# Decay products of an SSD head as two products of 64 targets, all eight heads of a tile in one run

## The chip, the cores and the metric

The kernel runs on one core of a Trainium2 chip. The metric is the device time of one execution in microseconds (us). The core's engines have instruction streams of their own: TensorE (PE in the profile, with its weight loads listed apart as PEld), VectorE (DVE), ScalarE (ACT), GpSimd (POOL) and SyncE (SP), which issues most of the DMAs. An engine takes its instructions in the order in which they stand; between engines, semaphores make one wait for another.

## The reference

A two-layer trunk over 256 positions and 2048 channels: layer 0 mixes with gated DeltaNet heads and band attention, layer 1 with Mamba-2 SSD heads, and each is followed by a squared-ReLU MLP. The change is in the SSD mixer. It has 64 heads of 64 channels in 8 groups; sequences are cut into chunks of 64 positions. The part that matters:

```python
acum = jnp.cumsum(dt * a, axis=2)
xdt = x * dt[..., None]
a_t = jnp.moveaxis(acum, 2, -1)
decay = jnp.exp(jnp.where(causal, a_t[..., :, None] - a_t[..., None, :], -jnp.inf))
cb = jnp.einsum('bnlgs,bnmgs->bnglm', cm, bm)
y_diag = jnp.einsum('bngelm,bnmgep->bnlgep', cb[:, :, :, None] * decay, xdt)
# a scan over the chunks adds y_off, then
y = y_diag + jnp.moveaxis(y_off, 0, 1) + x * d_skip.reshape(SSD_GROUPS, SSD_HPG, 1)
```

For each head, y_diag is a product of a matrix of weights (source position by target position: decay times cb) with the head's inputs (source position by 64 channels). All values are float32.

## The kernel before, in words

The 256 positions are handled as two tiles of 128, so the kernel's chunk is 128 positions where the reference's is 64; the formula allows either. Large projections run on TensorE all the time: their weights come in 1 MB pieces by DMA (`raw`, L499), ScalarE rounds each half to float32r (`wh`, L332), VectorE takes the remainder (`wl`, L336), and TensorE multiplies with both (L322). Between these products the code of a mixer is woven in.

`ssd_group` (L1378) is the code of one group of eight heads. It is a generator: each `yield` hands control back to the loop that emits the projections, so that a step of it is written every few products. It fetches the decay rows (`sE`, L1392, four heads in a [128, 4, 128] tile, four such tiles a group), computes cb (`scb`), transposes x (`sx`) and multiplies it by dt (L1437), and then works through four steps: tile 0 heads 4 to 7, tile 0 heads 0 to 3, and the same for tile 1. `weights` (L1415) makes the products' weights of one step out of a decay tile: a minimum on VectorE (L1418), four exponentials on ScalarE (L1420), the product with cb on VectorE (L1421). One step behind, the decay products of four heads run on TensorE: for each head, 128 source positions by 128 targets as weights, and as moving columns this head's 64 and, except for head 0, the 64 of the head before it, whose own product is written over that part next. All eight heads of a tile go into one PSUM tile `py`; behind head 0 VectorE adds the other terms and writes `y` (L1461, L1462). `ssd_gate` (L1466) reads `y` later.

`self.mm` (L325) is the call for all float32 products; a float32 product is two records of weight load and two of product in the profile. Other narrow products in the kernel: the cumulative sums of dt (L1357, float32, 64 weight columns, tile `sd_A`), the transposes of the 64 rows that come of it (`sd_rows`, L1365), and the dt projection (L667 and L668, float32r, by turns 128 and 64 weight columns, tile `wn`).

The order in which instructions stand on each engine is set when the program is built, by a scheduler that starts from the order of emission, the dependencies and the number of buffers of each pool. The pool of PSUM tiles `pm` has four, the pool of SBUF tiles that holds `sE`, `sx`, `scb` and others 18, `wl` five.

Of the kernel before, what the change touches and what calls it, by code (L numbers as in the profile page):

```python
# [14 lines left out]
ALU = mybir.AluOpType  # L15
# [3 lines left out]
P = 128  # L19
# [47 lines left out]
def wait(*tasks):  # L67
    for t in tasks:
        while not t.done:
            yield False  # L70
# [42 lines left out]
class Trunk:  # L113
# [933 lines left out]
    def gdn_tile(self, hg, t, kf, qf, vf, G):  # L1047
# [35 lines left out]
        self.mm(ps.rearrange("p h i -> p (h i)"), self.SU, gu.rearrange("p h i -> p (h i)"))  # L1083
        E = self.s2(tag="gE")
        nc.scalar.activation(E, ps, AF.Exp)
        nc.vector.tensor_tensor(E, E, self.row(self.U), op=ALU.mult)
        yield
# [12 lines left out]
        for h in range(4):  # L1100
            nc.vector.scalar_tensor_tensor(lt[:, h], ps[:, h], be[:, h : h + 1], E[:, h], op0=ALU.mult, op1=ALU.mult)

# [7 lines left out]
        p1 = self.s2(tag="gPt")  # L1110
        nc.vector.tensor_tensor(p1, ps, E, op=ALU.mult)
        G["Pt", t] = p1
# [265 lines left out]
    def ssd_group(self, g, xc, Bc, Cc, dtc):  # L1378

        nc = self.nc  # L1380
        yield from wait(xc, Bc, Cc, dtc())
        yield
        xf = xc.result
        H = slice(g * 8, g * 8 + 8)
        B, C = Bc.result[:, g % 4], Cc.result[:, g % 4]
        steps = [(t, hh) for t in range(2) for hh in (1, 0)]

        def decay(t, hh):

            E = self.s2(tag="sE")  # L1390
            h0 = g * 8 + hh * 4
            nc.scalar.dma_start(E, self.s_rows[t, h0 : h0 + 4].unsqueeze(0).to_broadcast([P, 4, P]))  # L1392
            return E

        Es = [decay(*n) for n in steps]
        ps = self.pm()
        for t in range(2):
            T = slice(t * P, t * P + P)
            self.mm(ps[:, t], B[:, T], C[:, T])
        self.mm(ps[:, 2], B[:, :P], C[:, P:])  # L1400
        cb = self.s2([P, 3, P], tag="scb")
        nc.vector.tensor_tensor(cb[:, :2], ps[:, :2], self.row(self.U, 2), op=ALU.mult)
        nc.scalar.copy(cb[:, 2], ps[:, 2])
        yield
        xt = []
        for t in range(2):
            ps = self.pm()
            for f in range(4):
                self.tr(ps[:, f], xf[:, f, t * P : t * P + P])
            x = self.s2([P, 8, 64], tag="sx")  # L1410
            nc.scalar.copy(x.rearrange("p h d -> p (h d)"), ps.rearrange("p f d -> p (f d)"))
            xt.append(x)
            yield

        def weights(t, hh, E):  # L1415

            h0 = g * 8 + hh * 4
            nc.vector.tensor_tensor(E, E, self.bc(self.s_col[:, t, h0 : h0 + 4]), op=ALU.min)  # L1418
            for h in range(4):
                nc.scalar.activation(E[:, h], E[:, h], AF.Exp, bias=self.s_ncol[:, t, h0 + h : h0 + h + 1])  # L1420
            nc.vector.tensor_tensor(E, E, self.row(cb[:, t]), op=ALU.mult)  # L1421
            return E


        xw = self.s2([P, 8, 64], tag="sxw")
        nc.vector.tensor_tensor(xw, xt[0], self.bc(self.s_dr[:, H], 64), op=ALU.mult)
        yield
        ps = self.pm([P, 8, 64])
        self.mm(ps.rearrange("p h d -> p (h d)"), cb[:, 2], xw.rearrange("p h d -> p (h d)"))
        yo = self.s2([P, 8, 64], tag="syo")  # L1430
        nc.vector.tensor_tensor(yo, ps, self.bc(self.s_ec[:, H], 64), op=ALU.mult)

        xds = []
        for t in range(2):
            xds.append(self.s2([P, 8, 64], tag="sxd"))
            nc.vector.tensor_tensor(xds[t], xt[t], self.bc(self.s_d[:, H], 64), op=ALU.mult)
            nc.vector.tensor_tensor(xt[t], xt[t], self.bc(self.dt[:, t, H], 64), op=ALU.mult)  # L1437
        y = self.unit(shape=[P, 2, 8, 64])
        yield
        py, E = None, None  # L1440
        for n in range(5):
            Ep = E
            if n < 4:
                E = weights(*steps[n], Es[n])
            if n == 0:
                yield
                continue
            t, hh = steps[n - 1]


            xf2 = xt[t].rearrange("p h d -> p (h d)")
            if hh == 1:
                py = self.pm([P, 512])
            for h in (3, 2, 1, 0):
                hl = hh * 4 + h
                s = slice(max(hl - 1, 0) * 64, hl * 64 + 64)
                self.mm(py[:, s], Ep[:, h], xf2[:, s])
            if hh == 0:
                xd = xds[t]
                if t == 1:  # L1460
                    nc.vector.tensor_tensor(xd, xd, yo, op=ALU.add)  # L1461
                nc.vector.tensor_tensor(y[:, t].rearrange("p h d -> p (h d)"), py, xd.rearrange("p h d -> p (h d)"), op=ALU.add)  # L1462
            yield
        return y

    def ssd_gate(self, g, ps, task):  # L1466
# [367 lines left out]
```

## Time and profile before

| | |
|---|---|
| time, median of 3 runs | 2707.59 us (2705.99 to 2708.86) |
| profiled execution | 2705.89 us |
| its span | 2704.0 us |
| mean granted TensorE clock | 0.993 |
| busy: PE, PEld, DVE | 2646.9, 2337.1, 2155.6 us |
| busy: ACT, POOL | 1348.6, 24.2 us |
| HBM read | 675.33 MB |
| decay products (`pm<-sx,sE`) on TensorE | from 1397.0 to 1828.9 us |

The profile is of one execution; its own time is 2705.89 us, of which 2704.0 are between the first and the last instruction. Products on TensorE are pipelined and their ends are modelled, so that records of products that follow each other overlap; how fast they go is read from their starts. In a row such as `L325 PE MATMUL pm<-sx,sE 128*128 128x64 f32`, `pm` is what is written, `sx` and `sE` what is read, 128*128 are rows and columns of the array that hold weights, and 128x64 are partitions and moving columns. The SSD groups lie in two places, four groups each, because the groups are worked through in two halves with an output projection behind each.

### The profile page before, as it was taken

How to read it: one execution, taken by the hardware profiler on the slowest of the kernel's cores; microseconds unless marked ns; L12 is line 12 of the kernel's file. 1: busy time of each engine (PE TensorE's matmuls, PEld its weight loads, DVE VectorE, ACT ScalarE, POOL GpSimd, SP SyncE). 2: the span in 40 equal slices, each digit the busy share in tenths (PEclk: the TensorE clock that was granted, in tenths of full speed). 3: DMA queues.
4: the chain of work that ended last, by engine and by line, in shares of the span. 5: the costliest groups of instructions: out<-in, count | busy, mean ns of one | idle time of the engine just before them, and what ended most of it. 6: DMA issues, size and time to landing. Idle time of an engine off the chain costs nothing.

```text
span 2704.0 us, 39515 instructions
## 1 busy us (share of the span) xinstructions
PE 2646.9 (98%) x15578; PEld 2337.1 (86%) x15578; DVE 2155.6 (80%) x3106; ACT 1348.6 (50%) x1990; POOL 24.2 (1%) x98
## 2 busy tenths in 40 slices
PE   5999999999999999999999999999999999999999
PEld 4887989888888888888888888888888888888888
DVE  7998998998888888889889876996787855555554
ACT  3444555455355354454556544655555354454452
POOL 1000000000000000000000000000000000000000
PEclk7999999999999999999999999999999999999999
DMA  9986487867899889988556665555557855555553
GB/s 350 354 326 235 169 313 266 317 248 284 315 348 329 334 326 334 331 326 300 181 182 212 224 234 203 203 179 180 196 187 290 323 201 190 187 187 187 188 193 133
DMA packets 100457, 680.05 MB, mean 251 GB/s; under 512 B 11184, under 2 KB 14512, under 8 KB 19376
## 3 DMA queue, kind: packets, MB, share of 16 engines
q1 hardware_dynamic: 95376, 669.07, 68.2%
q10 hardware_dynamic: 4896, 8.46, 1.1%
q8 instruction: 122, 2.00, 0.3%
q14 instruction: 63, 0.52, 0.1%
HBM read 675.33 MB, written 2.16 MB: 251 GB/s over the span
## 4 chain that ended last, share of the span: by engine, by line
PE 87%; DVE 7%; DMA 3%; ACT 2%; issue 1%; SPq 0%; ACTq 0%; DVEq 0%
PE pw L322 66%; PE pg L322 13%; PE pm L325 4%; PE pm L322 2%; DVE mraw L456 2%; DVE wl L336 2%; DMA mraw<-in_mod_dram 2%; PE pm L329 1%; DMA raw<-in_wo_ab_dram 1%; ACT wh L332 0%; DVE u L1614 0%; DVE hf L883 0%; DMA raw<-in_w_ab_dram 0%; DVE x L948 0%; ACT pm L1065 0%
## 5 line engine op out<-in xcount | busy, mean ns | idle before, releaser
L336 DVE TENSOR_TENSOR wl<-raw,wh 128x1024 fp32r<-128x1024 f32 x870 | 1051.0, 1220 | 440.0 <-ACT wh L332 437.3
L332 ACT CAST wh<-raw 128x1024 fp32r<-128x1024 f32 x870 | 905.6, 1051 | 991.4 <-PE pw L322 690.1
L322 PE MATMUL pw<-u,wh 128*128 128x512 f32 x5584 | 1321.2, 391 | 2.9 <-DVE x L948 1.5
L322 PEld LDWEIGHTS pw<-u,wh 128*128 128x128 f32 x5584 | 1031.7, 188 | 208.7 <-DVE x L948 1.5
L322 PEld LDWEIGHTS pw<-u,wl 128*128 128x128 f32 x5584 | 702.4, 191 | 22.7 <-issue 1.6
L322 PE MATMUL pw<-u,wl 128*128 128x256 f32 x5584 | 713.8, 283 | 1.5 <-DVE wl L336 0.7
L456 DVE SCALAR_TENSOR_TENSOR mraw<-mraw,crow 128x2048 f32<-128x2048 f32 x192 | 438.1, 2283 | 12.8 <-DMA mraw<-in_mod_dram 12.8
L322 PE MATMUL pg<-wh,u 128*128 128x512 f32 x864 | 281.8, 397 | 0.0
L322 PEld LDWEIGHTS pg<-wh,u 128*128 128x128 f32 x864 | 162.1, 188 | 32.3 <-issue 0.5
L948 DVE SCALAR_TENSOR_TENSOR x<-pw,mod,x 128x256 f32<-128x256 f32 x352 | 161.3, 478 | 32.7 <-PE pw L322 30.2
L322 PE MATMUL pg<-wl,u 128*128 128x512 f32 x432 | 169.6, 393 | 0.3
L322 PE MATMUL pg<-u,wh 128*128 128x256 f32 x672 | 124.5, 285 | 0.0
L322 PEld LDWEIGHTS pg<-u,wh 128*128 128x128 f32 x672 | 105.5, 192 | 0.3
L322 PEld LDWEIGHTS pg<-wl,u 128*128 128x128 f32 x432 | 81.3, 188 | 17.2 <-DVE wl L336 1.7
L322 PE MATMUL pg<-u,wl 128*128 128x256 f32 x336 | 95.5, 284 | 0.0
L322 PE MATMUL pm<-u,wh 128*128 128x256 f32 (+1 forms) x340 | 63.5, 291 | 19.2 <-ACT wh L332 19.2
L322 PEld LDWEIGHTS pm<-u,wh 128*128 128x128 f32 x340 | 53.9, 198 | 20.3 <-ACT wh L332 20.0
L322 PEld LDWEIGHTS pg<-u,wl 128*128 128x128 f32 x336 | 64.4, 192 | 0.0
L1007 DVE SCALAR_TENSOR_TENSOR u<-pad,cst,u 128x256 f32<-128x256 f32 x144 | 60.2, 477 | 4.4 <-ACT u L1001 4.3
L885 ACT ACTIVATE u<-hf,mod 128x256 fp32r<-128x256 f32 x64 | 29.3, 502 | 50.6 <-DVE hf L883 50.6
L1520 ACT COPY rs<-pw 128x512 f32<-128x512 f32 x64 | 36.9, 577 | 34.5 <-PE pw L322 34.5
L1526 ACT ACTIVATE rl<-rs 128x512 f32<-128x512 f32 x64 | 40.5, 633 | 23.7 <-DVE rs L1521 21.0
(298 smaller groups left out, 1556.0 us busy)
## 6 DMA issues: line engine op xcount, KB each, us to landing
raw<-in_w_dram SPq DMA_DIRECT2D x256, 1024.0 KB, 5.1
mraw<-in_mod_dram SPq DMA_DIRECT2D x192, 1024.0 KB, 6.2
raw<-in_w_ab_dram SPq DMA_DIRECT2D x56, 1024.0 KB, 5.4
raw<-in_w_ssd_dram SPq DMA_DIRECT2D x48, 1024.0 KB, 4.9
raw<-in_w_sz_dram SPq DMA_DIRECT2D x32, 1024.0 KB, 4.9
raw<-in_wo_ssd_dram SPq DMA_DIRECT2D x32, 1024.0 KB, 4.9
raw<-in_wo_ab_dram SPq DMA_DIRECT2D x16, 1024.0 KB, 7.0
sE<-sd_rowd ACTq DMA_DIRECT2D x32, 256.0 KB, 4.5
```

Of the source, the lines that this page charges most:

```text
L322: return self.nc.tensor.matmul(o, a, b, start=start, stop=stop, skip_group_check=True)
L325: self.nc.tensor.matmul(o, lhsT, rhs, start=True, stop=True, skip_group_check=True)
L329: return self.nc.tensor.transpose(o, a, self.anti if flip else self.ident[:k, :k])
L332: a = self.nc.scalar.copy(hi, src)
L336: b = self.nc.vector.tensor_tensor(lo, src, hi.bitcast(F32), op=ALU.subtract)
L456: x = nc.vector.scalar_tensor_tensor(raw, raw, 1.0, self.crow, op0=ALU.mult, op1=ALU.mult, accum_out=t[:, f : f + 1])
L885: nc.scalar.activation(hi, h[:, f], AF.Identity, bias=shift[:, col])
L948: self.last = nc.vector.scalar_tensor_tensor(x[:, 2 * b + f], ps[:, f, n], g[:, 2 * cb + f : 2 * cb + f + 1], x[:, 2 * b + f], op0=ALU.mul ...
L1007: nc.vector.scalar_tensor_tensor(h, pad[:, f, 1 + q : 257 + q], w[:, q, j : j + 1], h, op0=ALU.mult, op1=ALU.add)
L1520: nc.scalar.copy(lo, ps[:, :, 1])
L1526: nc.scalar.activation(rl, lo, AF.Relu)
```

## The change

The loop over five half-tile steps becomes a loop over the two tiles. For a tile it first makes the weights of heads 4 to 7 and then of heads 0 to 3, with a `yield` behind each as before. Then it takes a PSUM tile and writes the products of all eight heads in one run. Each head is two products: targets 0 to 63 and targets 64 to 127, each with all 128 sources, 64 weight columns and the head's 64 channels as moving columns. The first writes partitions 0 to 63 of `py`, the second partitions 64 to 127, which stand for the two column halves of the array. No head writes over another's columns any more. The y addition follows at once, in the same step, ahead of the weights of the next tile. The number of yields stays five.

```diff
         yield
-        py, E = None, None
-        for n in range(5):
-            Ep = E
-            if n < 4:
-                E = weights(*steps[n], Es[n])
-            if n == 0:
+        for t in range(2):
+            E = []
+            for hh in (1, 0):
+                E.insert(0, weights(t, hh, Es[2 * t + 1 - hh]))
                 yield
-                continue
-            t, hh = steps[n - 1]
-
-
-            xf2 = xt[t].rearrange("p h d -> p (h d)")
-            if hh == 1:
-                py = self.pm([P, 512])
-            for h in (3, 2, 1, 0):
-                hl = hh * 4 + h
-                s = slice(max(hl - 1, 0) * 64, hl * 64 + 64)
-                self.mm(py[:, s], Ep[:, h], xf2[:, s])
-            if hh == 0:
-                xd = xds[t]
-                if t == 1:
-                    nc.vector.tensor_tensor(xd, xd, yo, op=ALU.add)
-                nc.vector.tensor_tensor(y[:, t].rearrange("p h d -> p (h d)"), py, xd.rearrange("p h d -> p (h d)"), op=ALU.add)
-            yield
+            py = self.pm([P, 512])
+            for h in range(8):
+                c = slice(h * 64, h * 64 + 64)
+                for i in (slice(0, 64), slice(64, P)):
+                    self.mm(py[i, c], E[h // 4][:, h % 4, i], xt[t][:, h])
+            xd = xds[t]
+            if t == 1:
+                nc.vector.tensor_tensor(xd, xd, yo, op=ALU.add)
+            nc.vector.tensor_tensor(y[:, t].rearrange("p h d -> p (h d)"), py, xd.rearrange("p h d -> p (h d)"), op=ALU.add)
+        yield
         return y
```

TensorE in the first group of heads, tile 0, before. `pm` is the PSUM tile of the decay products, `sE` the weights (12880 heads 4 to 7, 12882 heads 0 to 3), `pw` the projection that runs meanwhile; the size is that of what is written, and x4 is four products.

```order
L322 MATMUL pw_13050<-u_12055,wh_12972 128x512 x3
L325 MATMUL pm_13035<-sx_12920,sE_12880 128x128 x4
L322 MATMUL pw_13050<-u_12055,wh_12972 128x512
L322 MATMUL pw_13050<-u_12056,wh_12972 128x512 x4
L325 MATMUL pm_13035<-sx_12920,sE_12882 128x128 x3
L325 MATMUL pm_13035<-sx_12920,sE_12882 128x64
L322 MATMUL pw_13050<-u_12088,wh_12976 128x512 x4
```

The same place now:

```order
L322 MATMUL pw_13045<-u_12055,wh_12972 128x512 x4
L322 MATMUL pw_13045<-u_12056,wh_12972 128x512 x4
L325 MATMUL pm_13054<-sx_12920,sE_12882 64x64 x8
L325 MATMUL pm_13054<-sx_12920,sE_12880 64x64 x8
L322 MATMUL pw_13045<-u_12088,wh_12976 128x512 x4
```

Two runs of four products became one run of sixteen, which stands where the second run stood; the first four heads moved behind five products of the projection, and heads 0 to 3 now come first.

TensorE in the same group, tile 1, before:

```order
L322 MATMUL pw_13050<-u_12089,wl_12977 128x256 x4
L325 MATMUL pm_13091<-sx_12942,sE_12884 128x128 x4
L322 MATMUL pw_13050<-u_12136,wl_13043 128x256 x4
L322 MATMUL pw_13050<-u_12137,wl_13043 128x256 x4
L322 MATMUL pw_13050<-u_12184,wl_13047 128x256 x3
L325 MATMUL pm_13091<-sx_12942,sE_12886 128x128 x3
L325 MATMUL pm_13091<-sx_12942,sE_12886 128x64
L322 MATMUL pw_13050<-u_12184,wl_13047 128x256
L322 MATMUL pw_13050<-u_12185,wl_13047 128x256 x4
```

and now:

```order
L322 MATMUL pw_13045<-u_12184,wl_13042 128x256 x4
L322 MATMUL pw_13045<-u_12185,wl_13042 128x256 x4
L322 MATMUL pw_13045<-u_12136,wh_13037 128x512 x4
L322 MATMUL pw_13045<-u_12137,wh_13037 128x512 x4
L325 MATMUL pm_13123<-sx_12942,sE_12886 64x64 x8
L325 MATMUL pm_13123<-sx_12942,sE_12884 64x64 x8
L322 MATMUL pw_13045<-u_12184,wh_13041 128x512 x4
```

The run of tile 1 moved behind the rest of the projection's 256-wide products and eight of its 512-wide ones.

VectorE between the weights of tile 0 and the y addition of tile 1, before (L1462 adds y, L1418 and L1421 are the two steps of the weights, L336 makes wl):

```order
L336 TENSOR_TENSOR wl_13043<-raw_13040,wh_13042 128x1024
L336 TENSOR_TENSOR wl_13047<-raw_13040,wh_13046 128x1024
L1418 TENSOR_TENSOR sE_12884<-sE_12884,sd_col 128x512
L1462 TENSOR_TENSOR u_12998<-pm_13035,sxd_12992 128x512
L996 TENSOR_TENSOR pad_13078<-pw_12906,cvt_13079 128x2x256
L1418 TENSOR_TENSOR sE_12886<-sE_12886,sd_col 128x512
L1421 TENSOR_TENSOR sE_12884<-sE_12884,scb_12892 128x512
L1007 SCALAR_TENSOR_TENSOR u_12895<-pad_13078,cst,u_12895 128x256 x4
L1421 TENSOR_TENSOR sE_12886<-sE_12886,scb_12892 128x512
```

and now (L1453 is the y addition):

```order
L336 TENSOR_TENSOR wl_13038<-raw_13035,wh_13037 128x1024
L336 TENSOR_TENSOR wl_13042<-raw_13035,wh_13041 128x1024
L1453 TENSOR_TENSOR u_12998<-pm_13054,sxd_12992 128x512
L1418 TENSOR_TENSOR sE_12884<-sE_12884,sd_col 128x512
L996 TENSOR_TENSOR pad_13086<-pw_12906,cvt_13087 128x2x256
L1418 TENSOR_TENSOR sE_12886<-sE_12886,sd_col 128x512
L1452 TENSOR_TENSOR sxd_12995<-sxd_12995,syo_12990 128x512
L336 TENSOR_TENSOR wl_13145<-raw_13142,wh_13144 128x1024
L1421 TENSOR_TENSOR sE_12884<-sE_12884,scb_12892 128x512
L1007 SCALAR_TENSOR_TENSOR u_12895<-pad_13086,cst,u_12895 128x256 x2
L1421 TENSOR_TENSOR sE_12886<-sE_12886,scb_12892 128x512
L1007 SCALAR_TENSOR_TENSOR u_12895<-pad_13086,cst,u_12895 128x256 x4
```

The y addition of tile 0 moved ahead of the first weights of tile 1, and one split (wl) moved ahead of their second step.

## The prediction

> **What bounds the kernel now.** I read the page first: busy time by engine, then the chain of work that ended last.
>
> ```profile
> PE 2646.9 (98%) x15578; PEld 2337.1 (86%) x15578; DVE 2155.6 (80%) x3106; ACT 1348.6 (50%) x1990; POOL 24.2 (1%) x98
> PE 87%; DVE 7%; DMA 3%; ACT 2%; issue 1%; SPq 0%; ACTq 0%; DVEq 0%
> ```
>
> TensorE is busy 98% of the span and carries 87% of the chain. That is an average, so next come the windows around the changed place: the decay products run from 1397 to 1829 us, four head groups in the first two windows and four in the last two. Two windows of the MLP behind them are added. The columns are window, its length, then busy time and instructions of PE, PEld, DVE, ACT and POOL, the granted clock, the DMA share and GB/s.
>
> ```profile
> 1390.00:1480.00 90.00, 90.00 (x526) 77.67 (x525) 88.67 (x137) 56.55 (x110) 0.62 (x6) 1.00 0.59 204
> 1480.00:1560.00 80.00, 79.70 (x390) 66.70 (x390) 67.06 (x114) 43.77 (x67) 0.00 (x0) 1.00 0.60 218
> 1560.00:1740.00 180.00, 180.00 (x1045) 158.93 (x1044) 135.48 (x197) 90.42 (x120) 0.72 (x7) 1.00 0.61 215
> 1740.00:1840.00 100.00, 100.00 (x568) 85.78 (x567) 90.07 (x143) 59.51 (x111) 0.31 (x3) 1.00 0.54 178
> ...
> 2150.00:2350.00 200.00, 200.00 (x1154) 177.11 (x1153) 117.00 (x133) 92.94 (x104) 0.00 (x0) 1.00 0.57 204
> 2350.00:2550.00 200.00, 200.00 (x1154) 177.14 (x1153) 111.89 (x124) 97.46 (x112) 0.00 (x0) 1.00 0.54 190
> ```
>
> Between 1390 and 1840 us TensorE idles for 0.3 us. So time on TensorE's stream there is time of the kernel, one to one. The rest of the program is filled by TensorE in the same way, with DMA at about half, so a gain here is not given back behind. One thing to watch is VectorE (DVE): 88.67 of 90 us in the first window. Busy time of pipelined products overlaps, so the price of a product has to come from starts, not from durations.
>
> **What a decay product costs now.** TensorE's rows in order of time in the first group, one row of its weight loads, and a piece of the chain:
>
> ```profile
> 1397.02 1.05 PE L325 MATMUL pm<-sx,sE 128*128 128x128 f32 x8
> 1397.83 1.39 PE L322 MATMUL pw<-u,wh 128*128 128x512 f32 x5
> 1399.06 1.00 PE L325 MATMUL pm<-sx,sE 128*128 128x128 f32 x8
> 1399.87 2.10 PE L322 MATMUL pw<-u,wh 128*128 128x512 f32 x8
> ...
> 1398.83 1.08 PEld L325 LDWEIGHTS pm<-sx,sE 128*128 128x128 f32 x8
> ...
> 1397.18 0.89 PE pm L325 x8
> ```
>
> One run is four products and x8 records: an fp32 product is two passes, each with its own weight load. The chain gives 0.89 us for eight passes, 0.111 each. All records of this product, by shape, and the narrow weight loads that the kernel has elsewhere:
>
> ```profile
> L325 PEld LDWEIGHTS pm<-sx,sE x256: 186/192/192, 1396.8 to 1828.9; 128*128 128x128 f32 x128
> L325 PE MATMUL pm<-sx,sE x256: 222/275/348, 1397.0 to 1828.9; 128*128 128x128 f32 x112, 128*128 128x64 f32 x16
> ...
> L322 PEld LDWEIGHTS pg<-u,wn 128*64 128x64 f32 x16 | 2.1, 134 | 0.0
> L325 PEld LDWEIGHTS pm<-Ucmask,sd_A 128*64 128x64 f32 x4 | 0.4, 136 | 0.5 <-DVE sd_A L1350 0.5
> ```
>
> 256 passes at 0.111 are **28.5 us**, which is all that the change can touch directly. The durations are min/median/max in ns. A product with 64 moving columns shows 222 where one with 128 shows 275: 64 columns are 53 ns of streaming. A load of 64 weight columns shows 134 to 136, one of 128 shows 192: 64 columns are about 56 ns of loading. Loading and streaming both take about 106 to 112 ns per pass now and lie over each other; that is the 0.111.
>
> **The change, part by part.** *Added passes.* Each head becomes two products of 64 weight columns and 64 moving columns, so 512 passes take the place of 256. One such pass alone needs 53 ns plus the 5 ns by which 0.111 exceeds 2 x 53: 58 ns. If the two halves of the array work at the same time, two passes fit in 58, so 29 ns each, 512 x 0.029 = 14.8 us. If passes still follow each other, 512 x 0.058 = 29.7 us. If load and product no longer overlap, 55 + 53 = 108 ns, 55.3 us. No row of this kernel shows two halves in use together: these are the bounds. I take 29 ns, with little confidence: the products of consecutive instructions share neither weights nor output partitions, and the only thing known to be common is the path of the loads.
>
> *Entering and leaving the narrow form.* The kernel has one fp32 product with 64 weight columns already, the cumulative sums of dt. TensorE's rows there, and then those of its weight loads:
>
> ```profile
> 1369.88 0.65 PE L325 MATMUL pm<-Ucmask,sd_A 128*64 128x128 f32 x4 [0.32 <-DVE sd_A L1350]
> 1370.46 1.22 PE L322 MATMUL pw<-u,wl 128*128 128x256 f32 x8
> 1371.61 0.33 PE L329 MATMUL pm<-ident,sd_rows 64*128 64x64 f32 x2
> ...
> 1370.46 1.01 PEld L322 LDWEIGHTS pw<-u,wl 128*128 128x128 f32 x8 [0.17 <-issue]
> ...
> 1401.80 2.07 PE L322 MATMUL pw<-u,wl 128*128 128x256 f32 x16
> 1403.71 1.06 PE L325 MATMUL pm<-sx,sE 128*128 128x128 f32 x8
> ```
>
> Of the row at 1369.88 the first load takes 0.056 (above) and four passes stream 128 columns each, 2 x 53 ns apiece: streaming ends near 1370.36. The next weight load, which waits for nothing that the profile shows, starts at 1370.46, nearly 0.1 later. Its eight products then take 1.22 us, where the steady rate of the row at 1401.80, 0.119 a pass, gives 1.12. So leaving costs 0.1 of nothing and 0.1 of a load that no product covers: about 0.20. Entering is seen at 1371.61 (a 64-row transpose): the row ahead ends at 1371.68 by its record, and a next product starts 0.07 ahead of that end, where in the steady row it starts 0.16 ahead (2.07 + 1401.80 - 1403.71); again 0.09, and then an uncovered load, 0.055 for 64 columns. Together **0.35 us for a run**. The old 128-wide runs pay none of it: 0.81 from 1397.02 to the next product at 1397.83. There are 16 new runs (8 groups, 2 tiles), so 5.6 us. The other bound is zero, from the dt projection, whose one-pass products alternate between 128 and 64 weight columns:
>
> ```profile
> 1338.96 3.90 PE L322 MATMUL pg<-u,wn 128*128 128x256 f32 x32
> 1342.69 0.63 PE L322 MATMUL pw<-u,wh 128*128 128x512 f32 x2
> ```
>
> 32 passes in 3.73 us are 0.117 each, the steady rate. I take 5.6, because the sums of dt are the same kind of product (fp32, two passes) and the projection is not. The Trainium skill ("TensorEngine Tiling (Array Packing)", Key Properties) says that changing the tiling mode drains TensorE: the sums of dt agree with it, the projection's row does not, and by the rule every change of width would pay, which leaves the sum at 5.6.
>
> *Moved work.* Heads of one tile now run together, so the first four wait for the last four. In the first group the run of tile 0 stands behind eight 512-wide products instead of three, that of tile 1 behind all 32 of the 256-wide ones and eight 512-wide. VectorE, same place:
>
> ```profile
> 1396.95 0.68 DVE L1421 TENSOR_TENSOR sE<-sE,scb 128x512 f32<-128x512 f32 x1
> ...
> 1404.41 0.68 DVE L1421 TENSOR_TENSOR sE<-sE,scb 128x512 f32<-128x512 f32 x1
> ...
> 1405.92 1.00 PE L325 MATMUL pm<-sx,sE 128*128 128x128 f32 x8
> ```
>
> Weights of tile 0 are done at 1397.63; its run starts five 512-wide products behind 1397.02, which is 1.23 (1397.83 to 1399.06), so near 1398.2. Weights of tile 1 were done at 1405.1; the y addition and one split now stand ahead of them on VectorE (0.6 and 1.2 us), so 1406.9. Its run starts behind five more 256-wide products than the second old run (0.6) and eight 512-wide ones (1.9, from 1399.87 to 1401.80), so about 2.4 us after 1405.92, near 1408.3. No wait on TensorE: 0. The y addition of tile 1 is the reverse: VectorE reaches it about when that run ends, and what stands behind it are the splits of the next weights (wl) and the next group's masks. That can cost VectorE about 1 us a group. It would first have to use up the lead that wl has over its first use. The least that I find between 1390 and 1480 us is this split, done at 1465.01 and used at 1468.66:
>
> ```profile
> 1463.79 1.22 DVE L336 TENSOR_TENSOR wl<-raw,wh 128x1024 fp32r<-128x1024 f32 x1
> ...
> 1468.66 0.40 PE L322 MATMUL pg<-wl,u 128*128 128x512 f32 x1
> ```
>
> That is 3.6 us, against about 1 us in each of the three groups up to there. I put it at 0, at most 1 us.
>
> *Sum:* 14.8 + 5.6 - 28.5 = **-8.1 us**. The profiled execution took 2705.9 us (span 2704.0), so 2697.8; the median of the three runs is 1.7 above the profiled one: **2699.5**.
>
> **The rivals.**
>
> *Passes in turn (slower).* The loads of the two halves go one after the other on one path, as they do now. Place: the weight loads inside the 16 runs; price 58 ns a pass, 29.7 + 5.6 - 28.5 = +6.8 us, 2714.4. It decides as soon as a pass costs more than (28.5 - 5.6) / 512 = 45 ns. For it: in every row today a load starts only when the product ahead has started. Against: with one set of spare weights that is seen either way.
>
> *Half of it.* Loads partly side by side, 43.5 ns a pass: 22.3 + 5.6 - 28.5 = -0.6, 2707.0. The work is halved and the runs' edges eat it.
>
> *No overlap of load and product.* 108 ns a pass: 55.3 + 5.6 - 28.5 = +32.4, 2740.0. Against: the eight loads from 1398.83 lie under products that use all rows. The Trainium skill ("TensorE: Matmul & The Clock Gate", Part 3) says a load overlaps products in flight only where the row groups differ, and both halves use all rows; the trace disagrees for full-width products, and no run here shows the halves. The same part reports 2.38 times for three column tiles, which is for the forecast.
>
> *Edges cost nothing*, as in the dt projection: 14.8 - 28.5 = -13.7, 2693.9.
>
> **How the numbers follow.** Forecast 0.36 (2699.5, its own range 2697 to 2703 for 28 to 36 ns a pass), edges free 0.06, half 0.17, in turn 0.33, no overlap 0.08. What this kernel can tell from no change is about 0.2%, 5.4 us. Faster is the forecast and the free edges, 0.42. Within 0.2% is the half and a little of the passes in turn, 0.19; slower the rest, 0.39. The range takes in all but the last rival and the tails: 2692 to 2718.
>
> **What would show it.** In the changed kernel's trace TensorE's run of a tile should hold 32 records of 64-wide form. From its first start to the next wide product, about 1.0 us means halves at once, about 1.9 means in turn, 3.5 no overlap. The first wide load behind each run should start with a gap of 0.09. TensorE's waits for sE should stay at none, and VectorE's for the y addition should be the only new ones. The forecast is wrong if a pass costs over 45 ns, or if wl comes late on TensorE between 1390 and 1480 us.

## The result and the profile after

The changed kernel takes 2697.5 us (median of 5 runs, 2696.3 to 2699.49) against 2706.27 for the kernel before on the same chip (5 runs, 2704.61 to 2708.86): a ratio of 0.9964 with a 95% interval of 0.9953 to 0.9975, or 8.8 us less, 6.8 to 12.7 by the interval. The profiled execution has a span of 2695.8 us where the one before had 2704.0, which is 8.2 less. The forecast was 8.1 less, 2699.5 us; of the 2.0 us by which it is off, 1.3 lie in the time of the kernel before, of which it knew a median of 2707.59.

The page's busy times by engine and its chain of work, of the changed kernel:

```profile
PE 2638.6 (98%) x15834; PEld 2325.0 (86%) x15834; DVE 2154.2 (80%) x3106; ACT 1348.0 (50%) x1990; POOL 24.4 (1%) x98
PE 91%; DVE 5%; DMA 1%; ACT 1%; issue 1%; SPq 0%; ACTq 0%; DVEq 0%
```

TensorE has 256 more records of product and 256 more of weight load, as expected of 512 passes in place of 256, and is busy 8.3 us less. Still 98% busy, it bounds the kernel as before. The windows around the changed place, in the columns of the prediction:

```profile
1390.00:1480.00 90.00, 89.87 (x637) 75.19 (x637) 87.89 (x136) 56.07 (x107) 0.62 (x6) 1.00 0.58 203
1480.00:1560.00 80.00, 79.56 (x430) 65.75 (x429) 70.28 (x118) 45.47 (x75) 0.00 (x0) 1.00 0.64 235
1560.00:1740.00 180.00, 180.00 (x1089) 158.66 (x1088) 135.27 (x198) 90.95 (x118) 0.73 (x7) 1.00 0.60 213
1740.00:1840.00 100.00, 100.00 (x671) 83.19 (x670) 90.95 (x144) 60.89 (x114) 0.31 (x3) 1.00 0.53 187
```

TensorE idles for 0.57 us in them, where it was 0.30. So the time went out of its stream and not out of waits. TensorE's products in order of time in the first group, then its weight loads at the first run:

```profile
1393.69 5.40 PE L322 MATMUL pw<-u,wh 128*128 128x512 f32 x23
1399.01 1.15 PE L325 MATMUL pm<-sx,sE 128*64 128x64 f32 x32
1400.10 2.11 PE L322 MATMUL pw<-u,wh 128*128 128x512 f32 x8
1402.04 4.00 PE L322 MATMUL pw<-u,wl 128*128 128x256 f32 x32
1405.88 2.00 PE L322 MATMUL pw<-u,wh 128*128 128x512 f32 x8
1407.81 1.15 PE L325 MATMUL pm<-sx,sE 128*64 128x64 f32 x32
1408.89 2.11 PE L322 MATMUL pw<-u,wh 128*128 128x512 f32 x8
...
1399.01 1.01 PEld L325 LDWEIGHTS pm<-sx,sE 128*64 128x64 f32 x32 [0.35 <-ACT cvt L995]
1400.09 1.69 PEld L322 LDWEIGHTS pw<-u,wh 128*128 128x128 f32 x8
```

A run holds 32 passes and takes 1.09 us from its first start to the next product of the projection (1399.01 to 1400.10); before, eight passes took 0.81, and a tile had two such runs. All records of the decay products, their count, min/median/max of the durations in ns, and the shape, whose count is of a sample of every third record:

```profile
L325 PEld LDWEIGHTS pm<-sx,sE x512: 132/138/138, 1399.0 to 1821.5; 128*64 128x64 f32 x171
L325 PE MATMUL pm<-sx,sE x512: 222/222/271, 1399.0 to 1821.5; 128*64 128x64 f32 x171
```

The durations are those of narrow forms in the profile before (134 to 136 for a load of 64 columns, 222 for a product with 64 moving columns): a pass has not become shorter, two of them stand side by side. In the starts of the single records of the first run the weight loads come in pairs, at 1399.012 and 1399.019, 1399.067 and 1399.074, 1399.124 and 1399.130 and so on: the second of a pair 6 to 7 ns behind the first, and one pair every 58 ns. That is 29 ns a pass.

To follow the gain along the program, the start of the same product of the projection was compared in the two traces. From 1392 us, ahead of the first run, to 1842, behind the last, the changed kernel gains 8.1 us; from there to the end 0.9 more. That is one wait that went: near 2083 us TensorE of the kernel before waits for ScalarE to round `u` (0.68 of idle time), and in neither profile of the changed kernel does it. Why it went was not taken apart. Ahead of 1392, where nothing changed, two profiled executions of this same kernel lie 0.8 and 3.3 us behind the one before, so single spans are good to some 3 us and the stretch is the better measure.

### The profile page after: what moved, and what is told of

The parts are those of the page before. It is cut to its first block, busy times and chain, and to the rows that moved or that the text cites. A ratio compares the mean times of both kernels' runs of the same rounds, so it can differ in the third digit from the quotient of the medians.

```text
span 2695.8 us, 40020 instructions
## 1 busy us (share of the span) xinstructions
PE 2638.6 (98%) x15834; PEld 2325.0 (86%) x15834; DVE 2154.2 (80%) x3106; ACT 1348.0 (50%) x1990; POOL 24.4 (1%) x98
## 4 chain that ended last, share of the span: by engine, by line
PE 91%; DVE 5%; DMA 1%; ACT 1%; issue 1%; SPq 0%; ACTq 0%; DVEq 0%
PE pw L322 71%; PE pg L322 13%; PE pm L325 3%; PE pm L322 2%; DVE mraw L456 2%; PE pm L329 1%; DVE wl L336 1%; DMA mraw<-in_mod_dram 1%; DVE u L1605 0%; ACT wh L332 0%; DVE hf L883 0%; DMA raw<-in_w_ab_dram 0%; DVE u L886 0%; DMA x<-in_x_dram 0%; DMA sd_rowd<-sd_rows 0%
## 5 line engine op out<-in xcount | busy, mean ns | idle before, releaser
L336 DVE TENSOR_TENSOR wl<-raw,wh 128x1024 fp32r<-128x1024 f32 x870 | 1050.8, 1220 | 435.9 <-ACT wh L332 433.1
L1512 DVE TENSOR_TENSOR rs<-pw,rs 128x512 f32<-128x512 f32 x64 | 43.8, 684 | 10.0 <-ACT rs L1511 10.0
```

The lines of the kernel that those rows point to most:

```text
L336: b = self.nc.vector.tensor_tensor(lo, src, hi.bitcast(F32), op=ALU.subtract)
L1512: nc.vector.tensor_tensor(lo, ps[:, :, 0], lo, op=ALU.add)
```

## The experiments

They change `ssd_group` of the changed kernel, except two: the halves in runs of four heads start from the kernel before, and the last one changes the dt projection. To compare runs of different length, each run is priced in the same way, from the starts of single records: from the last 512-wide product of the projection ahead of it to the second one behind it, less the 0.46 us that two such products take at their steady rate (eight in 1.93 from 1405.88, with the 0.10 gap ahead of the run in it, is 0.229 each). Before, a run of eight passes costs 0.892 by this (1.352 less 0.46), 28.5 us for 32; in the changed kernel a run of 32 costs 1.275, 20.4 us for 16. Runs between 256-wide products, priced with 0.119 for each of those, cost the same (0.897 and 1.275).

### The same regrouping with products of full width

All eight heads of a tile in one run, each head one product of 128 targets and its own 64 channels; no column halves.

```diff
-                for i in (slice(0, 64), slice(64, P)):
-                    self.mm(py[i, c], E[h // 4][:, h % 4, i], xt[t][:, h])
+                self.mm(py[:, c], E[h // 4][:, h % 4], xt[t][:, h])
```

> The changed kernel, but each head is one product of all 128 targets and 64 moving columns; the run of eight heads and the order of the work stay. If two halves of the array working at once make the gain: back to the time before, 2706 (256 passes at 0.111 = 28.5 us, bound by the load of 128 weight columns, and no edges), within 2 us. If it comes from the regrouping into one run or from the moved additions: 2698, as the changed kernel. If it comes from moving 64 columns in place of 128: under 2700 as well, and starts of passes 58 ns apart in the trace in place of 111.

Measured: 2706.06 us against 2706.39, ratio 1.000 (0.9991 to 1.001). TensorE's first run:

```profile
1397.70 1.89 PE L325 MATMUL pm<-sx,sE 128*128 128x64 f32 x16
1399.40 2.10 PE L322 MATMUL pw<-u,wh 128*128 128x512 f32 x8
```

16 passes take 1.70 us to the next product. In the starts of single records one follows the other every 0.112 us, as before: the load of 128 columns sets that pace and not the stream, which is half as long now. The run costs 1.786, twice the 0.892 of eight passes. So the regrouping and the halved moving columns, without the halves, are worth nothing by the runs' prices, and at most 2.4 us by the times; what gains is the halves.

### The halves one after the other

The same products, all eight lower halves of a tile first and then the eight upper ones.

```diff
-            for h in range(8):
-                c = slice(h * 64, h * 64 + 64)
-                for i in (slice(0, 64), slice(64, P)):
+            for i in (slice(0, 64), slice(64, P)):
+                for h in range(8):
+                    c = slice(h * 64, h * 64 + 64)
```

> The changed kernel with the same 16 products a run in another order: the lower half of all eight heads, then the upper half of all eight. If the gain is two halves at once and the queue doesn't look eight products ahead: passes 58 ns apart, 1.9 us a run in place of 1.0, about 0.85 x 16 = 13.5 us over the changed kernel, 2711. If narrower products are what gains, in whichever order: 2697.5, starts 29 ns apart on average.

Measured: 2708.7 us against 2706.39, ratio 1.001 (1.0001 to 1.0019).

```profile
1399.94 1.90 PE L325 MATMUL pm<-sx,sE 128*64 128x64 f32 x32
1401.77 2.11 PE L322 MATMUL pw<-u,wh 128*128 128x512 f32 x8
```

The same 32 records, in 1.83 us and not 1.09. Passes of one half start 58 ns apart. This is the rival "passes in turn" as a kernel: a pass costs the 58 ns that it was priced at, the kernel is slower than before, and the change escapes it only because the two halves alternate. The run is a little below 32 in turn (32 x 0.058 and the 0.15 of leaving are 2.01): in the starts of single loads a second series sets in at 1400.690, when two of the first sixteen are still to come, and three passes overlap. That is 0.18 a run, and it takes the rival's 6.8 us down to 3.9.

### Each product twice

Every product is written a second time, which changes nothing in the output.

```diff
-                for i in (slice(0, 64), slice(64, P)):
+                for i in (slice(0, 64), slice(64, P)) * 2:
```

> The changed kernel with each product written twice (lower, upper, lower, upper of each head; the second pair repeats the first). Measures the price of a pass in time: 512 passes more. At 29 ns: +14.8 us over the changed kernel, 2712. At 58: +29.7, 2727. If the runs are hidden behind something else: under +5, 2702.

Measured: 2709.8 us against 2706.39, ratio 1.001 (1.0001 to 1.002); 12.2 us more than the changed kernel's difference.

```profile
1394.98 2.09 PE L325 MATMUL pm<-sx,sE 128*64 128x64 f32 x64
1397.00 2.11 PE L322 MATMUL pw<-u,wh 128*128 128x512 f32 x8
```

64 passes take 2.02 and 32 take 1.09: 32 more passes in 0.93, which is 29 ns each. This is the marginal price of a pass, free of the run's edges. By the runs' cost (2.208 each) the kernel should be 6.8 us slower than before; the time says 3.4, at most 5.4 by the interval. The traces show what lies between them. In the stretch from 1392 to 1842 the kernel loses 5.6: 6.8 for the runs, less 0.5 for waits that the kernel before has in four of its runs and this one does not have, less 0.46 for the kernel before's wait at 1499, which it does not have either (both are shown further below), is 5.8. Behind 1842 it loses 0.9 less, by the same wait at 2083 that went in the changed kernel. That leaves 4.7, inside the interval. Ahead of 1392, where nothing changed, this execution is 3.3 us early.

### Halves in runs of four heads

The loop of the kernel before, with its 32 runs of four heads, but two half products for a head.

```diff
-                s = slice(max(hl - 1, 0) * 64, hl * 64 + 64)
-                self.mm(py[:, s], Ep[:, h], xf2[:, s])
+                s = slice(hl * 64, hl * 64 + 64)
+                for i in (slice(0, 64), slice(64, P)):
+                    self.mm(py[i, s], Ep[:, h, i], xf2[:, s])
```

(The removed lines are those of the kernel before.)

> The loop of before, two runs of four heads a tile, with the products of the change in it. 16 runs more, so 16 edges more. If entering and leaving cost 0.35 us a run: +5.6 us over the changed kernel, 2703. If edges cost nothing: 2697.5. If the places of the runs matter more than their edges (weights come late, as in the kernel before): over 2705.

Measured: 2703.9 us against 2706.39, ratio 0.9992 (0.9983 to 1.0002).

```profile
1397.53 0.69 PE L325 MATMUL pm<-sx,sE 128*64 128x64 f32 x16
1398.15 1.42 PE L322 MATMUL pw<-u,wh 128*128 128x512 f32 x5
```

A run of 16 passes takes 0.62 to the next product and costs 0.810. With the changed kernel's 1.275 for 32, a pass is 29.1 ns once more, and what is left of a run without its passes, 1.275 less 32 x 0.0291, is **0.344 us** for entering and leaving. The prediction had 0.35. Sixteen more runs at that price take 5.5 of the 8.1 us: in the old grouping the halves alone would hardly have been seen, and the regrouping, worth nothing by itself, is what pays for the halves' edges.

### The changed kernel again, and both tiles in one run

If edges cost 0.34 a run, half as many runs should gain 2.75 us. In the last kernel of this group all four steps of weights come first, then one run of 32 products, tile 1 ahead of tile 0, and then both y additions (left out of the cut below). Its companion is the changed kernel, once more.

```diff
+        Ew = {}
         for t in range(2):
-            E = []
             for hh in (1, 0):
-                E.insert(0, weights(t, hh, Es[2 * t + 1 - hh]))
+                Ew[t, hh] = weights(t, hh, Es[2 * t + 1 - hh])
                 yield
-            py = self.pm([P, 512])
+        pys = [self.pm([P, 512]) for _ in range(2)]
+        for t in (1, 0):
             for h in range(8):
...
-                    self.mm(py[i, c], E[h // 4][:, h % 4, i], xt[t][:, h])
+                    self.mm(pys[t][i, c], Ew[t, h // 4][:, h % 4, i], xt[t][:, h])
```

> The changed kernel itself, as the partner of the next kernel on the same chip: 2697.5, 0.9964 of before.

> The changed kernel with both tiles of a group in one run of 32 products (tile 1 first); weights of all four steps are made before it. 8 runs in place of 16, so 8 edges fewer. If an edge costs 0.35 us: 2.8 us under the changed kernel, 2694.7. If the later run delays VectorE's additions and with them wl or the gates: no gain, or over 2697.5, with waits of TensorE for wl or u in the trace. If edges are free: 2697.5.

Measured, against 2706.14: the changed kernel 2697.79 us, ratio 0.9967 (0.9955 to 0.9979); both tiles in one run 2695.48 us (2693.03 to 2696.65), ratio 0.9958 (0.9946 to 0.9971). TensorE's run of the first group:

```profile
1406.50 2.09 PE L325 MATMUL pm<-sx,sE 128*64 128x64 f32 x64
1408.52 1.88 PE L322 MATMUL pw<-u,wh 128*128 128x512 f32 x7
```

Eight runs of 2.208 are 17.7 us, 10.8 less than before, and 10.7 were measured. By the medians it is 2.3 us ahead of the changed kernel, near the 2.75 of the edges; the two intervals overlap, so that this step rests on the runs' lengths more than on the times. It has the lowest median of this study.

The runs' costs and the times side by side, in us against the kernel before:

| kernel | runs | cost of one | sum less 28.5 | measured (95%) |
|---|---|---|---|---|
| changed | 16 | 1.275 | -8.1 | -8.8 (-12.7 to -6.8) |
| changed, again | 16 | 1.275 | -8.1 | -8.4 (-12.2 to -5.7) |
| full width, one run | 16 | 1.786 | +0.1 | -0.3 (-2.4 to +2.7) |
| halves in turn | 16 | 2.025 | +3.9 | +2.3 (+0.3 to +5.1) |
| each product twice | 16 | 2.208 | +6.8 | +3.4 (+0.3 to +5.4) |
| halves, four heads | 32 | 0.810 | -2.6 | -2.5 (-4.6 to +0.5) |
| both tiles in one run | 8 | 2.208 | -10.8 | -10.7 (-14.6 to -7.8) |

### What the edges hang on

The prediction saw two cases that disagree: the sums of dt pay for the narrow form, the dt projection does not. They differ in more than one thing. Here the dt projection's narrow product is made in float32, two passes, as the sums of dt are; its neighbours stay float32r and 128 wide. The same line makes a projection of layer 0, which is changed with it; nothing else is.

```diff
-                self.mmx(o[:width, :SEQ], w[:, :width], u[:, k % 2, 1], False, k == 15)
+                self.mmx(o[:width, :SEQ], w[:, :width].bitcast(F32), u[:, k % 2, 1].bitcast(F32), False, k == 15)
```

> The changed kernel; in the dt projection (and the gates' projection) the narrow product of each step is float32 in place of float32r, with the same 64 (16) weight columns, so that it alternates with float32r products of 128 (32) columns. If it is the float32 form that makes the switch cost, the 32 switches in the dt projection show the gap of 0.09 us and an uncovered load each, and the 32 products take about 16 x (0.117 + 0.44 + 0.35) = 14.5 us in place of 3.7. If only what follows decides (a change of width as such), 16 x (0.117 + 0.44) = 8.9 us and no gaps.

Measured, one run: 2715.68 us. The projection in TensorE's products, in this kernel, and some of its weight loads there:

```profile
1347.91 14.24 PE L322 MATMUL pg<-u,wn 128*128 128x256 f32 x48
1362.09 3.93 PE L322 MATMUL pw<-u,wh 128*128 128x512 f32 x16
...
1347.69 0.19 PEld L322 LDWEIGHTS pg<-u,wn 128*128 128x128 f32 x1
1348.12 0.19 PEld L322 LDWEIGHTS pg<-u,wn 128*64 128x64 f32 x2 [0.24 <-issue]
1348.70 0.51 PEld L322 LDWEIGHTS pg<-u,wn 128*128 128x128 f32 x3 [0.39 <-issue]
1349.59 0.50 PEld L322 LDWEIGHTS pg<-u,wn 128*128 128x128 f32 x3 [0.39 <-issue]
```

14.18 us from 1347.91 to 1362.09, where it was 3.73. A float32 pass with 256 moving columns is four times the 53 ns of 64, so the products alone would take 16 x (0.117 + 2 x 0.212) = 8.7. The other 5.5 are 16 times in and out: 0.34 a time, the price of the changed kernel's runs. In the starts of single records a round of one wide and one narrow product takes 0.89, and the next load starts 0.096 behind the end of the streaming ahead of it, on the way in and on the way out. So it is not the width alone (the float32r projection pays nothing) and not float32 alone (the old 128-wide runs pay nothing): it takes a narrow float32 product next to another form. The projection of layer 0, by turns with 32 and 16 weight columns, took 3.64 us before and now:

```profile
225.45 12.37 PE L322 MATMUL pg<-u,wn 128*32 128x256 f32 x48
237.75 7.13 PE L322 MATMUL pg<-raw,hw 128*128 128x512 f32 x16
```

12.30 us less 8.7 are 3.6, 0.23 a time: the two gaps of 0.096 are 0.19, and what is left is two uncovered loads that are shorter for 16 and 32 columns. The two projections together take 19.1 us more than before, and this one run lies 17.9 us above the changed kernel on the same chip. Which property of the narrow float32 form does it (the form itself or the array's division) was not taken apart further.

## Why the prediction was right

**The price of a pass** was the term with the least confidence: 29 ns if the halves work at once, 58 if in turn, and it decided the sign. It is 29.2 (twice as many passes) and 29.1 (half as many a run). The forecast's condition, that two passes fit into the 58 ns of one, is what the pairs of records show. Its test, about 1.0 us for a run, came out at 1.09. One of its figures was a slip: the low end of its own range, 2697, does not follow from 28 ns, by which the sum gives 2699.0.

The Trainium skill ("TensorE: Matmul & The Clock Gate", Part 3) says that a weight load overlaps products in flight only where the row groups differ. The trace differs: both halves use all 128 rows, and the loads of one half start 6 to 7 ns behind those of the other and under its products. The Trainium skill's other page ("TensorEngine Tiling (Array Packing)", Key Properties) says that different tiles load and multiply in parallel; by that rule the sum is the forecast's, and the trace agrees.

**Passes in turn** (0.33) did not happen in this kernel, but they are real: with the halves in blocks the run takes 1.83. The argument for this rival was that all loads share one path. They don't wait on it for each other when they go to different halves.

**Half of it** (22.3 for the passes) and **no overlap** (55.3) have no trace in any run: 14.8 was predicted for the passes and 512 x 0.0291 = 14.9 measured. **Free edges** fell too, for 0.344 a run, 5.5 us, stood where 5.6 were taken. The step that carried this was to trust the sums of dt (float32) over the projection (float32r), and the projection made in float32 shows that to be the right distinction. Its gap of 0.09 behind a run is there: the last narrow pass starts at 1399.944, streams for 54 ns, and the next load starts at 1400.094, 0.096 later.

**Moved work** was put at 0, at most 1 us. Its total is small, as said, but three details failed. VectorE was to wait about 1 us a group for the y addition of tile 1; the group of all eight y additions from 1390 to 1500 us, and the one new wait of VectorE in that window, of the changed kernel:

```profile
L1453 DVE TENSOR_TENSOR u<-pm,sxd 128x512 f32<-128x512 f32 x8 | 5.5, 684 | 0.0
...
DVE sE L1421 <- ACT sE L1420: 1.5, 3, 0.7
```

The addition waits 0.0: by the time VectorE comes to it the run has ended. The prediction had VectorE there too early. What waits instead are three products with cb, for their exponentials, 1.5 us in all.

The second detail is that TensorE was to wait for no `sE`. It does at two of the sixteen runs, in both profiles of the changed kernel. VectorE's product with cb and TensorE's run at the second of them:

```profile
1490.15 0.69 DVE L1421 TENSOR_TENSOR sE<-sE,scb 128x512 f32<-128x512 f32 x1
...
1490.36 0.61 PE L322 MATMUL pg<-wh,u 128*128 128x512 f32 x2
1490.98 1.15 PE L325 MATMUL pm<-sx,sE 128*64 128x64 f32 x32
```

The weights are done at 1490.83, and the first load starts 0.12 behind that. The run costs 1.358 and not 1.275; the one at 1456.58, whose weights are done at 1456.43, costs 1.475. Together that is 0.3 us. One of VectorE's three waits, 0.54 at 1488.34, lies just ahead of the wait at 1490.98; at 1456 VectorE is at a 2.29 us step for `mraw` until it comes to the weights.

The third is a place that the prediction didn't look at, the gate behind the four groups. Its transposes before, and then in the changed kernel, where there are two:

```profile
1498.94 0.61 PE L322 MATMUL pg<-wh,u 128*128 128x512 f32 x2
1499.86 0.30 PE L329 MATMUL pm<-ident,u 128*128 128x128 f32 x1 [0.30 <-DVE u L1491]
```

```profile
1503.99 0.39 PE L322 MATMUL pg<-wh,u 128*128 128x512 f32 x1
1504.50 0.41 PE L329 MATMUL pm<-ident,u 128*128 128x128 f32 x2
...
1518.81 0.61 PE L322 MATMUL pg<-wh,u 128*128 128x512 f32 x2
1519.73 0.30 PE L329 MATMUL pm<-ident,u 128*128 128x128 f32 x1 [0.30 <-DVE u L1482]
```

By the starts, TensorE loses 0.46 at 1499 before, and 0.28 and 0.46 now. So the changed kernel gives back 0.28 there: in the starts of the same products it is 3.11 us ahead of the kernel before at 1498, ahead of all transposes, and 2.83 at 1560. The other profile of the changed kernel and four of the five other kernels that change these products give back 0.3 to 0.4 (the one with each product twice has none of these waits and gains 0.5). In VectorE's order of time six splits of weights (wl) stand between the last y addition and the scaling of the gate's `u`, where there were three, and the scaling comes at 1503.87 and not at 1499.22. The halves in runs of four heads, whose loop is that of the kernel before, have the same six, so it is not the regrouping that moves the scaling; what does was not taken apart.

**The sum.** From 1392 to 1842 us: 8.1 gained by the runs; 0.5 gained, because four runs of the kernel before cost 0.98 to 1.04 and not 0.892 (at the first, 1426.17, the first load starts 0.12 behind the end of VectorE's product of x and dt) and no run of the changed kernel waits for that; 0.3 lost by the two runs that wait for `sE`; and 0.3 lost at the gate. That is -8.0, and -8.1 is what the traces show. The two large terms were right, each to 0.1 us. That the small ones, which the forecast did not have, cancel is luck, and the 0.9 at 2083 is outside it: 8.1 was forecast against 8.8 measured, inside the interval.

## What to carry to other kernels

Where a small fp32 product loads 128 columns and streams no more than that, split it into the two column halves and alternate them instruction by instruction; in blocks of one half after the other there is no gain. Then make few, long runs of it: entering and leaving the narrow float32 form cost 0.34 us here, as much as 12 passes, and put together with the split the regrouping was worth 5.5 of the 8.1 us. A form that another data type has for nothing is no bound for this one: look for the case in the trace that agrees in type, passes and width.

## What was not expected

- Passes of the two halves start 6 to 7 ns apart. Whatever their loads share costs no more than that here.
- TensorE does not take its products strictly in the order in which they stand. It brings passes of the other half forward, but not far: with eight products of one half ahead, only the last three of its sixteen passes overlap with the upper half (1.83 us for the run, 2.01 if none did, 1.09 if all).
- The gap is about 0.096 us each way, for 64 weight columns as for 16, and in these runs only with narrow float32 products: 0.34 a time beside 128-wide products and 0.23 beside 32-wide ones. The difference is the first load, which nothing covers.
